# Loading the attention output matrix as two half loads, 64 rows outermost, in a two-layer hybrid kernel

## The chip, the cores and the metric

The program runs on one core of a Trainium2 chip. TensorE multiplies matrices, VectorE and ScalarE read its results out of PSUM, GpSimd (POOL) does elementwise work from SBUF, and SyncE (SP) only issues transfers; ScalarE issues transfers too, between its own instructions. Sixteen DMA engines carry all transfers. Every engine runs its instructions in their written order and waits on semaphores. The metric is the device time in microseconds. Each of the kernels is timed in several runs, and one execution is taken with the hardware profiler.

## What is computed

Two layers act on 2048 latent tokens and 256 context tokens of width 1024. Layer 0 is windowed attention with 16 heads of 64 and a SiLU gate, layer 1 a bidirectional diagonal state-space layer with a gated output. The matrix of this document, `w_out` of layer 0, is used in one line of the reference, after the attention:

```
q, k, v, z = jnp.split(h @ w_in, [...], axis=-1)
p = jax.nn.softmax(jnp.concatenate([s_win, s_ctx, s_sink], axis=-1), axis=-1)
o = (jnp.einsum('bnkgqj,bnjkd->bnqkgd', p[..., :nw], vw)
     + jnp.einsum('bnkgqc,bckd->bnqkgd', p[..., nw:nw + n_ctx], vc))
y = (o * jax.nn.silu(z)) @ w_out
```

## The kernel before

All matrix products are made of three float32r products of split operands: each tile is split into a high part, made by a copy (line 106 on ScalarE, 108 on VectorE), and a low part, the difference (line 111 on GpSimd or VectorE). A scheduler sets each engine's order of instructions when the program is built; the transfers of SyncE and ScalarE share eight completion semaphores, so a transfer also waits for an earlier one that holds its semaphore.

Phase 1 (up to about 590 us) walks over units of `w_in`: for each unit of 256 columns (keys, values, queries, gate) a raw tile `wraw` is loaded and split, and 24 products per output tile (lines 116 to 118, tile `mm`, four PSUM buffers) run over chunks of 384 tokens. ScalarE takes the gate tiles `z` out of PSUM (line 574) and stores them to `zd`. Beside the last units VectorE and ScalarE compute the tables of layer 1 (`pwe`, `pwg`, lines 240 to 380), which are stored to `tabd` with waits in between. Phase 2 is the attention: keys `kall` and `kctx`, queries `qta` and `qtb`, values `vt` and `vc` are loaded again from HBM, scores `S` (line 898) go through mask and maximum on VectorE (line 911), the exponential on ScalarE (line 912), a scaling on GpSimd (line 933), transposes on TensorE (line 947), a split (951, 952) and the product with the values (`ov`, line 967). The output product with `w_out` (line 1009) fills TensorE between these.

`w_out` is taken in eight tiles of 128 rows by 1024 columns. Rows of a tile are not adjacent in HBM: tile `kt` holds 64 rows of one head on its upper 64 partitions and 64 rows of another head, 256 rows further, on the lower 64. `wo_src` (line 491) builds this view of HBM with dimensions 2, 1, 64 and 1024: the outermost one counts the two heads. One transfer moves a whole tile, or half of its columns. The tiles are loaded at three places, always from SyncE:

- Four tiles of 512 KB into `wraw`, by `wo_early` at line 638, in two pairs between the loads of the last two units. ScalarE makes their high parts into `hhl` (three) and `adaq` (one), GpSimd the low parts.
- Two tiles of 512 KB into `wor`, also at line 638, between the loads of mask and sink and those of `qtb` and `kall`. ScalarE copies them into `wraw`.
- Two tiles as four transfers of 256 KB into `ogh` and `ogl`, at line 816, after the first gate tiles `zt` of phase 2 and ahead of `x`, `gate` and the next values. ScalarE copies them into `whi` and `wlo`, GpSimd and VectorE make the low parts.

ScalarE runs these copies in order with the reads of PSUM that TensorE waits for.

Of the kernel before, what the change touches and what calls it, by code (L numbers as in the profile page):

```python
# [16 lines left out]
D = 1024  # L17
# [68 lines left out]
class Net:  # L86
# [401 lines left out]
                self.split(hv, lv, raw[:, s].rearrange("p k (e f r) -> p f k e r", e=n, f=2)[:, f], "v", lo_eng)  # L488
        return hi, lo

    def wo_src(self, kt):
        wo = self.a["attn_w_out"][0].rearrange("(v a g d) n -> a d v g n", v=2, a=2, g=4, d=64)
        return wo[:, :, kt // 4, kt % 4]

    def phase1(self):
        nc, a = self.nc, self.a
# [3 lines left out]
        with ExitStack() as es:  # L500
# [27 lines left out]
            h = {}  # L528
# [104 lines left out]
            def wo_early(slots, raw=None):  # L633
                if raw is None:
                    raw = pb.tile([128, KT, 256], F32, name="wraw", bufs=2).rearrange("p k c -> p (k c)")
                for j, (hi, lo) in enumerate(slots):
                    c = slice(j * D, (j + 1) * D)
                    nc.sync.dma_start(raw[:, c], self.wo_src(len(self.wo)))
                    self.split(hi, lo, raw[:, c], "a", "g")
                    self.wo.append((hi, lo))  # L640

# [40 lines left out]
            for n, (half, (kind, x)) in enumerate(units):  # L682
# [25 lines left out]
                if n == 17:  # L708
                    t = pb.tile([128, 2, KT, CH], F32R, name="hhl2").rearrange("p a k c -> p (a k c)")
                    s2 = [[t[:, (j * 2 + i) * D:(j * 2 + i + 1) * D] for i in range(2)] for j in range(3)]  # L710
                    wo_early(s2[:2])
                if n == 18:
                    t = pb.tile([128, 2, 4, 256], F32R, name="adaq", bufs=1).rearrange("p a k c -> p a (k c)")
                    wo_early([s2[2], [t[:, 0], t[:, 1]]])
                    self.ada_cols(1, sm, self.ada_ps(ps2), self.g1, self.s1)
                    esm.close()
                    wts[19] = w_of(19)
                    for c in chunks:
                        if c == 5:
                            self.zlate = v_later(c, w) + z_later(c, wts[19], 3)  # L720
                        else:
                            if c == 3:
                                v_unit([c], w)
                            z_unit([c], wts[19], 3, False)
                            if c == 4:
                                v_unit([c], w)
                        if c == 3:
                            e3.close()
                            self.phase2_keys(zp)
                            pst = es.enter_context(self.pool("p1st"))  # L730
                            ts = [pb.tile([128, KT, 256], F32R, name="wraw", bufs=2).rearrange("p k c -> p (k c)") for _ in range(2)]
                            wo_early([(t[:, 0:D], t[:, D:2 * D]) for t in ts], pst.tile([128, 2 * D], F32, name="wor"))
                    break
# [54 lines left out]
    def phase2(self):  # L788
        nc, a = self.nc, self.a
        kall, pb = self.kall, self.pb  # L790
        with ExitStack() as es:
# [14 lines left out]
            def wtile(name, shape, dt, n):  # L806
                i = turn[name] = turn.get(name, -1) + 1
                return late[0].tile(shape, dt, name=f"{name}{i % n}", bufs=1)
# [3 lines left out]
            def load_wo(kt):  # L812
                for h in range(2):
                    t = wtile(("ogh", "ogl")[h], [128, 4, 128], F32R, 4).bitcast(F32).rearrange("p a b -> p (a b)")
                    wraw[kt, h] = t
                    nc.sync.dma_start(t, self.wo_src(kt)[:, :, h * 512:(h + 1) * 512])

            def split_wo(kt):
                t = pb.tile([128, KT, 256], F32R, name=("whi", "wlo")[kt - 6])
# [212 lines left out]
            def open_late():  # L1032
                while zlate:
                    fill(1)
                self.esd.close()
                late.append(es.enter_context(self.pool("p2l", 1)))
                for nm in LO.split():
                    late[0].tile([128, sizes.get(nm[:2], 512)], F32, name=nm, bufs=1)
                load_z(2, 0)
                load_z(2, 1)  # L1040
                for kt in range(6, KT):
                    load_wo(kt)
                load_x(2)
                for r in range(2):
                    gates[r] = wtile("gate", [128, D], F32, 2)
                    nc.sync.dma_start(gates[r], dap(self.modd[0], r * 3 * D + 2 * D, [[0, 128], [1, D]]))
# [975 lines left out]
```

## Time and profile before

| | us |
|---|---|
| median of three runs | 2732.37 (2731.87 to 2736.12) |
| profiled execution | 2733.07 |
| span of its instructions | 2731.3 |
| TensorE busy in the span | 2545.3 (93%) |
| VectorE, ScalarE, GpSimd busy | 1621.8, 1187.9, 938.6 |
| mean granted TensorE clock | 0.970 |

The profiled execution's own time is 1.8 us over its span. A granted clock of 1.00 is 2.4 GHz and 0.50 is 1.2 GHz. In the timeline, the idle time of an engine ahead of an instruction and what ended it stand in square brackets; an entry such as ACTq or SPq is a transfer being issued, not the transfer. A wait is put down to what came last by the profile. The row of a stretch gives its bounds and length, then the busy time (with the count of instructions) of TensorE's products, TensorE's weight loads, VectorE, ScalarE and GpSimd, the granted clock, the mean busy share of the 16 DMA engines, and GB/s.

### The profile page before, as it was taken

The page shows a single profiled execution, that of the slowest core. Times are in us where ns is not written, and L with a number is a line of the kernel's source. Part 1 is how long each engine was busy: PE and PEld are TensorE (multiplying, and loading weights), DVE is VectorE, ACT ScalarE, POOL GpSimd, SP SyncE. Part 2 cuts the span into 40 slices and gives each one's busy share as a digit, 9 for nine tenths or more (in the row PEclk, how much of TensorE's full clock was granted, in tenths as well). Part 3 has the DMA queues.
Part 4 walks back from the last instruction along what each step waited for, and adds up shares of the span by engine and source line. Part 5 has one row for each costly group of instructions (what it writes and reads, how often), then busy time and mean ns, then how long its engine had stood idle before and what let it go on. Part 6 is the DMA issues. An engine that isn't in the chain of part 4 may idle for free. (4 is left out here: it accounts for less than half of the span.)

```text
span 2731.3 us, 43882 instructions
## 1 busy us (share of the span) xinstructions
PE 2545.3 (93%) x15973; PEld 2279.4 (83%) x15973; DVE 1621.8 (59%) x3816; ACT 1187.9 (43%) x2711; POOL 938.6 (34%) x778
## 2 busy tenths in 40 slices
PE   7999999975799999999899999999679999999998
PEld 5999989875688899999799988889657778888887
DVE  4763377513798888888732168699986440001454
ACT  3201310123677777777644347734179830001221
POOL 0312332102445445455522154256255231212121
PEclk9999999988899999999999999999889999999999
DMA  8555446355454444344273100245223332223542
GB/s 281 169 170 149 151 151 179 116 149 147 106 132 108 106 101 112 85 111 101 89 191 105 63 24 24 76 135 162 80 71 96 103 84 67 80 62 99 180 146 85
DMA packets 374030, 317.22 MB, mean 116 GB/s; under 512 B 63910, under 2 KB 327094, under 8 KB 373814
## 3 DMA queue, kind: packets, MB, share of 16 engines
q1 hardware_dynamic: 264422, 235.64, 31.0%
q10 hardware_dynamic: 109392, 78.76, 9.0%
q8 instruction: 127, 2.08, 0.3%
q14 instruction: 89, 0.73, 0.1%
HBM read 225.63 MB, written 88.70 MB: 115 GB/s over the span
## 5 line engine op out<-in xcount | busy, mean ns | idle before, releaser
L116 PE MATMUL mm<-hhl,whi 128*128 128x384 f32 x848 | 288.2, 343 | 8.6 <-ACT z L574 4.1
L117 PE MATMUL mm<-hhl,whi 128*128 128x384 f32 x848 | 288.2, 340 | 0.4 <-POOL hhl L111 0.4
L933 POOL TENSOR_SCALAR P<-P,ri 128x640 f32<-128x640 f32 (+2 forms) x272 | 208.5, 780 | 230.9 <-DVE ri L931 190.0
L118 PE MATMUL mm<-hhl,wlo 128*128 128x384 f32 x848 | 286.3, 338 | 0.0
L952 DVE TENSOR_TENSOR pl<-pt,ph 128x512 fp32r<-128x512 f32 (+1 forms) x384 | 233.1, 607 | 37.8 <-ACT ph L951 34.0
L911 DVE CUSTOM_DVE_ANT_0 P<-S,mask,sink 128x640 f32<-128x640 f32 (+1 forms) x240 | 209.0, 871 | 58.1 <-PE S L902 52.4
L951 ACT ACTIVATE ph<-pt 128x512 fp32r<-128x512 f32 (+1 forms) x384 | 202.6, 528 | 75.2 <-PE pt L947 72.5
L947 PE MATMUL pt<-ident,P 128*128 128x128 f32 x1312 | 213.5, 276 | 11.9 <-POOL P L933 7.0
L912 ACT ACTIVATE P<-P,nm 128x640 f32<-128x640 f32 (+1 forms) x256 | 208.1, 813 | 22.2 <-DVE nm L911 6.6
L947 PEld LDWEIGHTS pt<-ident,P 128*128 128x128 f32 x1312 | 157.8, 141 | 30.0 <-POOL P L933 13.1
L116 PEld LDWEIGHTS mm<-hhl,whi 128*128 128x128 f32 x848 | 160.4, 190 | 19.6 <-issue 10.8
L111 POOL TENSOR_TENSOR wlo<-wraw,whi 128x512 fp32r<-128x512 f32 x60 | 86.6, 1471 | 258.9 <-DVE whi L108 252.7
L117 PEld LDWEIGHTS mm<-hhl,whi 128*128 128x128 f32 x848 | 161.2, 190 | 7.1 <-issue 6.1
L118 PEld LDWEIGHTS mm<-hhl,wlo 128*128 128x128 f32 x848 | 160.9, 190 | 0.8 <-issue 0.4
L117 PE MATMUL zps<-zh,wzh 128*128 128x256 f32 x512 | 146.0, 286 | 5.3 <-POOL zh L111 5.3
L116 PE MATMUL zps<-zh,wzh 128*128 128x256 f32 x512 | 145.8, 286 | 2.4 <-ACT wzh L106 1.1
L1851 DVE TENSOR_TENSOR gy<-gps,gs 128x512 f32<-128x512 f32 x32 | 22.1, 691 | 208.4 <-POOL gs L1849 208.4
L118 PE MATMUL zps<-zh,wzl 128*128 128x256 f32 x512 | 145.6, 285 | 0.0
L1424 DVE TENSOR_TENSOR sall<-sall 128x64 f32<-128x64 f32 x560 | 137.5, 301 | 0.1
L1848 ACT ACTIVATE gs<-gps 128x512 f32<-128x512 f32 x32 | 19.1, 596 | 259.6 <-PE gps L118 259.6
L967 PE MATMUL ov<-ph,vt 128*128 128x256 f32 x368 | 98.3, 283 | 21.9 <-DVE oT L979 21.9
L111 POOL TENSOR_TENSOR zh<-zraw,zh 128x512 fp32r<-128x512 f32 x61 | 81.9, 1350 | 101.1 <-ACT zh L106 77.8
(591 smaller groups left out, 7703.8 us busy)
## 6 DMA issues: line engine op xcount, KB each, us to landing
qta<-qd SPq DMA_DIRECT2D x144, 128.0 KB
qtb<-qd SPq DMA_DIRECT2D x144, 128.0 KB
wraw<-in_w_ada_dram SPq DMA_DIRECT2D x16, 1024.0 KB
zraw<-h1d SPq DMA_DIRECT2D x64, 256.0 KB
wraw<-in_attn_w_in_dram SPq DMA_DIRECT2D x12, 1024.0 KB
mq<-qqd SPq DMA_DIRECT2D x64, 192.0 KB
qd<-oh ACTq DMA_DIRECT2D x48, 192.0 KB
qd<-ol ACTq DMA_DIRECT2D x48, 192.0 KB
```

The source lines that it names most:

```text
L111: (nc.gpsimd if lo_eng == "g" else nc.vector).tensor_tensor(lo, src, hi.bitcast(F32), op=OP.subtract)
L116: nc.tensor.matmul(ps, whi(k), mhi(k), start=first and k == 0, stop=False)
L117: nc.tensor.matmul(ps, whi(k), mlo(k), start=False, stop=False)
L118: nc.tensor.matmul(ps, wlo(k), mhi(k), start=False, stop=last and k == nk - 1)
L911: nc.vector.tensor_tensor_reduce(o, sc, mk, -0.125, nsink[:, h:h + 1], OP.add, OP.min, nm)
L912: nc.scalar.activation(p, p, AF.Exp, bias=nm, scale=-1.0, accum_out=SM[i][:, e:e + 1])
L933: (nc.vector if e >= CTXV else nc.gpsimd).tensor_scalar(P[i][e], P[i][e], ri[:, e:e + 1], 1.0, op0=OP.mult, op1=OP.mult)
L947: ins = nc.tensor.transpose(t[:, c - c0], P[i][e][:, k * 128:(k + 1) * 128], self.ident)
L951: nc.scalar.activation(ph[:, c0:c1], t, AF.Copy)
L952: nc.vector.tensor_tensor(pl[:, c0:c1], t, ph[:, c0:c1].bitcast(F32), op=OP.subtract)
L967: self.keep("D", nc.tensor.matmul(o, v, ph[:, k * n:(k + 1) * n], start=k == 0, stop=False))
L1424: nc.vector.tensor_add(y[:, :, hs[h]], t[:, h, i], y[:, :, hs[h]])
```

## The change

Each load of a `w_out` tile is issued as two transfers, one for the upper and one for the lower 64 partitions. The view of HBM of each has 64 rows outermost. The bytes, their places in SBUF and the readers stay the same; ten transfers become twenty.

```diff
-    def wo_src(self, kt):
+    def load_wo(self, dst, kt, c):
         wo = self.a["attn_w_out"][0].rearrange("(v a g d) n -> a d v g n", v=2, a=2, g=4, d=64)
-        return wo[:, :, kt // 4, kt % 4]
+        for a in range(2):
+            self.nc.sync.dma_start(dst[a * 64:(a + 1) * 64], wo[a, :, kt // 4, kt % 4, c])
...
-                    nc.sync.dma_start(raw[:, c], self.wo_src(len(self.wo)))
+                    self.load_wo(raw[:, c], len(self.wo), slice(0, D))
...
-                    nc.sync.dma_start(t, self.wo_src(kt)[:, :, h * 512:(h + 1) * 512])
+                    self.load_wo(t, kt, slice(h * 512, (h + 1) * 512))
```

Lines after 495 stand one line later in the changed file. The scheduler orders the program anew. On SyncE, in phase 1, the two pairs of `wraw` loads stand between the loads of the value unit (`wraw_4976`) and of the last gate unit; before:

```order
L649 DMA wraw_4976<-in_attn_w_in_dram 128x8x256
L638 DMA wraw_4983<-in_attn_w_out_dram 128x1x1024 x2
L655 DMA wraw_5160<-in_attn_w_in_dram 128x8x128 x2
L638 DMA wraw_5172<-in_attn_w_out_dram 128x1x1024 x2
L655 DMA wraw_5193<-in_attn_w_in_dram 128x8x128 x2
```

and now, at the same place:

```order
L650 DMA wraw_4976<-in_attn_w_in_dram 128x8x256
L494 DMA wraw_4983<-in_attn_w_out_dram 64x1024 x4
L656 DMA wraw_5162<-in_attn_w_in_dram 128x8x128 x2
L494 DMA wraw_5174<-in_attn_w_out_dram 64x1024 x4
L656 DMA wraw_5197<-in_attn_w_in_dram 128x8x128 x2
```

Two transfers became four in each pair, and nothing else moved. On SyncE at the start of phase 2, from the mask (`z_5373`) to the keys, before:

```order
L768 DMA z_5373<-in_k_mask_dram 128x256
L772 DMA sink_5377<-in_attn_sink_dram 128x16
L638 DMA wor_5385<-in_attn_w_out_dram 128x1x1024 x2
L786 DMA qtb_5354<-qd_57 32x8x128 x8
L779 DMA kall_5351<-kd_58 32x4x384 x14
L834 DMA vt2_5552<-vd_59 128x512
L834 DMA vt3_5554<-vd_59 128x512
L834 DMA vc_5556<-vd_59 128x512
L834 DMA vc_5558<-vd_59 128x512
L779 DMA kall_5351<-kd_58 32x4x384 x2
```

and now:

```order
L769 DMA z_5377<-in_k_mask_dram 128x256
L773 DMA sink_5381<-in_attn_sink_dram 128x16
L494 DMA wor_5389<-in_attn_w_out_dram 64x1024 x4
L787 DMA qtb_5358<-qd_57 32x8x128 x8
L780 DMA kall_5355<-kd_58 32x4x384 x6
L835 DMA vt2_5558<-vd_59 128x512
L835 DMA vt3_5560<-vd_59 128x512
L835 DMA vc_5562<-vd_59 128x512
L835 DMA vc_5564<-vd_59 128x512
L780 DMA kall_5355<-kd_58 32x4x384 x10
```

The four loads of values moved ahead of eight of the loads of keys. On ScalarE, where the last four pieces of `w_out` are copied (`whi`, `wlo`) among the exponentials of the first block of phase 2, before:

```order
L106 ACTIVATE whi<-ogh_5933 128x512
L951 ACTIVATE ph<-pt 128x512
L912 ACTIVATE P,sm<-P,nm 128x512
L106 ACTIVATE whi<-ogl_5935 128x512
L106 ACTIVATE wlo<-ogh_5937 128x512
L106 ACTIVATE wlo<-ogl_5939 128x512
L951 ACTIVATE ph<-pt 128x512
L978 ACTIVATE oc<-ov 64x256
```

and now:

```order
L106 ACTIVATE whi<-ogh_5939 128x512
L952 ACTIVATE ph<-pt 128x512
L913 ACTIVATE P,sm<-P,nm 128x512
L106 ACTIVATE whi<-ogl_5942 128x512
L106 ACTIVATE wlo<-ogh_5945 128x512
L952 ACTIVATE ph<-pt 128x512
L979 ACTIVATE oc<-ov 64x256
L106 ACTIVATE wlo<-ogl_5948 128x512
```

The last copy moved behind one split and one read of the value product. TensorE's order differs in two rows of the later gate projection, GpSimd's not at all; VectorE's differs at these places and, with the same instructions, around the scan of layer 1.

## Rows read from the trace of the kernel before

**Rows 1.** Page, GB/s moved in 40 slices of the span.

```profile
GB/s 281 169 170 149 151 151 179 116 149 147 106 132 108 106 101 112 85 111 101 89 191 105 63 24 24 76 135 162 80 71 96 103 84 67 80 62 99 180 146 85
```

**Rows 2.** Stretches: busy time by engine, granted clock, DMA share, GB/s.

```profile
500.00:706.00 206.00, 139.11 (x825) 133.74 (x823) 75.77 (x225) 57.36 (x108) 35.36 (x28) 0.83 0.48 140
524.00:529.00 5.00, 3.73 (x22) 3.41 (x20) 4.93 (x27) 0.00 (x0) 0.00 (x0) 1.00 0.13 52
706.00:760.00 54.00, 53.16 (x376) 49.36 (x374) 48.12 (x129) 43.33 (x105) 27.94 (x32) 1.00 0.35 90
1955.00:1990.00 35.00, 1.01 (x8) 0.81 (x7) 35.00 (x216) 1.54 (x3) 1.40 (x2) 0.55 0.03 12
```

**Rows 3.** TensorE's waits between 500 and 706 us: total, times, longest.

```profile
PE S L898 <- DVE nm L911: 18.5, 1, 18.5
PE ov L967 <- DVE oT L979: 17.7, 2, 16.6
PE mm L116 <- ACT z L574: 16.5, 3, 9.4
PE pt L626 <- DVE pl L952: 5.2, 1, 5.2
PE pt L947 <- POOL P L933: 4.0, 2, 3.8
PE mm L116 <- DVE whi L108: 3.6, 1, 3.6
```

**Rows 4.** ScalarE's timeline, copies of `w_out`: start, duration, idle before.

```profile
530.30 1.06 ACT L106 ACTIVATE hhl<-wraw 128x1024 fp32r<-128x1024 f32 x1 [9.07 <-DMA wraw<-in_attn_w_out_dram]
...
562.74 1.06 ACT L106 ACTIVATE adaq<-wraw 128x1024 fp32r<-128x1024 f32 x1 [9.14 <-DMA wraw<-in_attn_w_out_dram]
...
623.13 1.06 ACT L106 ACTIVATE wraw<-wor 128x1024 fp32r<-128x1024 f32 x1 [10.30 <-DMA wor<-in_attn_w_out_dram]
633.74 1.06 ACT L106 ACTIVATE wraw<-wor 128x1024 fp32r<-128x1024 f32 x1 [9.55 <-DMA wor<-in_attn_w_out_dram]
...
679.74 0.63 ACT L106 ACTIVATE whi<-ogh 128x512 fp32r<-128x512 f32 x1 [4.37 <-DMA ogh<-in_attn_w_out_dram]
...
697.46 0.63 ACT L106 ACTIVATE wlo<-ogl 128x512 fp32r<-128x512 f32 x1 [5.85 <-DMA ogl<-in_attn_w_out_dram]
```

**Rows 5.** SyncE's timeline: when transfers are issued, time until the last issue.

```profile
2.63 1.03 SPq L199 DMA_DIRECT2D adaw<-in_w_ada_dram  x2
...
506.32 1.13 SPq L638 DMA_DIRECT2D wraw<-in_attn_w_out_dram  x2
...
606.26 1.56 SPq L638 DMA_DIRECT2D wor<-in_attn_w_out_dram  x2
608.51 26.45 SPq L786 DMA_DIRECT2D qtb<-qd  x8
...
670.76 0.54 SPq L816 DMA_DIRECT2D ogh<-in_attn_w_out_dram  x1
```

**Rows 6.** TensorE's timeline: first use of a load; end of a pause.

```profile
8.06 1.93 PE L166 MATMUL adap<-adaw,cs 128*32 128x256 f32 x16 [2.99 <-DMA adaw<-in_w_ada_dram]
...
638.07 0.58 PE L898 MATMUL S<-kall,qta 128*128 128x256 f32 x1 [18.45 <-DVE nm L911]
```

**Rows 7.** VectorE's timeline: splits of weights, and the mask.

```profile
529.94 2.35 DVE L111 TENSOR_TENSOR wlo<-wraw,whi 128x1024 fp32r<-128x1024 f32 x2
...
586.92 1.42 DVE L108 CAST whi<-wraw 128x512 fp32r<-128x512 f32 x4
...
611.62 0.23 DVE L769 CAST mask<-z 128x128 bf16<-128x128 f32 x1 [19.86 <-DMA z<-in_k_mask_dram]
```

**Rows 8.** Sums over half-clock stretches, three up to 583 us, four after.

```profile
sum 17.10, PE 11.53 PEld 11.53 DVE 7.56 ACT 8.84 POOL 5.31; mean PE 3.84 PEld 3.84 DVE 2.52 ACT 2.95 POOL 1.77
...
sum 54.60, PE 19.88 PEld 18.82 DVE 19.47 ACT 16.75 POOL 13.74; mean PE 4.97 PEld 4.71 DVE 4.87 ACT 4.19 POOL 3.43
```

**Rows 9.** A wait of ScalarE between 500 and 710 us.

```profile
ACT P L912 <- DMA kall<-kd: 6.0, 1, 6.0
```

## The prediction

> **What bounds the kernel now.** I read the page first, then the busy time by stretches, TensorE's waits, and the timelines of ScalarE and SyncE at the three places that load `w_out`. From 706 us on TensorE is busy 53.16 of 54 us; between 500 and 706 us it works only 139.11 of 206, at a mean granted clock of 0.83 [rows 2]. So this stretch, the seam of phases 1 and 2, loses 66.9 us to idling. Its waits name ScalarE, VectorE and GpSimd, not transfers [rows 3]; the transfers stand one step further back. ScalarE runs in order, and at each copy of a `w_out` tile it stands still until the tile has landed: 9.07 us at 530.30, 9.14 at 562.74, 10.30 and 9.55 at 623.13 and 633.74, and four waits of 3.3 to 5.9 us between 675.4 and 697.46, of which the first and last are shown [rows 4]. Behind it wait the reads of PSUM, and so TensorE.
>
> Why these loads are late: two tiles issued at 606.26 are usable at 623.13 and 633.74 [rows 4, 5], 10.6 us apart, so 512 KB moves at 49 GB/s. Between 524 and 529 us, when little but such a load moves, the DMA share is 0.13 at 52 GB/s [rows 2], and 0.13 is 2 of 16 engines. The view has outermost dimension 2. The other loads of the kernel have 32 or more rows outermost, and the first slice moves 281 GB/s [rows 1]. Transfers behind them suffer as well: the eight `qtb` loads, issued from 608.51, take 26.45 us to get out [rows 5], because part of each queues on the two busy engines and holds its semaphore.
>
> **What the change does to a load.** With 64 rows outermost on both sides I expect each half to spread over all 16 engines. Price of a 16-engine load that the trace shows: two loads of 1 MB are issued from 2.63 and the first is in use at 8.06 [rows 5, 6], so 1 MB takes at most 5.4 us from issue to use, and 1.05 MB at 281 GB/s takes 3.7. A pair of tiles is 1.05 MB. I take 5.4 for a pair on an idle queue and 3.7 behind other work; before, the first pair took 530.30 - 506.32 = 24.0. Below, a pair cannot go under the 3.7; above, the price of before stays the bound.
>
> The Trainium skill speaks on both sides here. Its page "DMA: Bandwidth & Descriptors", section "Rules for kernel authors", says that a transfer split into two partition halves gains nothing, since both halves run on the same engines; the same section says that an outermost dimension smaller than 16 confines a transfer to that many engines. The share of 0.13 agrees with the second. By the first the time would stay at 2732, which is a rival below.
>
> **The sum, place by place.** Times are positions in the trace of before.
>
> Place 1, `wraw`. The first pair now lands by about 512, so the wait of 9.07 us at 530.30 goes [rows 4]. The second pair is written over a raw tile whose last split on VectorE ends at 529.94 + 2.35 = 532.3 [rows 7]; it can be issued then, and lands at 532.3 + 5.4 = 537.7. From its last copy (562.74, [rows 4]) to the split that gives TensorE the last gate unit's weights (586.92, [rows 7]) runs a chain of table work, its stores and VectorE: 24.2 us. I let it run at the same length: 537.7 + 24.2 = 561.9 instead of 586.92, 25.0 earlier. Cross-check: TensorE's waits here are 16.5 + 3.6 = 20.1 [rows 3], and of 11.53 us of work at half clock half can come back, 5.8 [rows 8], 25.9 in all. So a pause of 1 to 2 us stays, where the table chain takes the place of the load. I take 24.
>
> Place 2, `wor`. The mask, issued just ahead, is in use at 611.62 [rows 7], so what is queued before is then through; 3.7 more for the pair gives 615.3 instead of 633.74. TensorE restarted at 638.07 after 18.45 us [rows 6], 4.3 after the last copy began; 615.3 + 4.3 is 619.6, just where it had stopped. As TensorE gains up to 3 us of clock on SyncE on the way there, I leave 2.5 of the 18.5: 16. The next wait, 5.2, stands behind ScalarE's 6.0 us at a store that needs the semaphore of a `kall` load [rows 3, 9]. The queue no longer starts 25 us late, but it still has 26 loads to move, so I leave 1.3: 3.9. Here the new order helps too: the values, needed first, stand ahead of eight key loads.
>
> Place 3, `ogh` and `ogl`. ScalarE wants the first piece at 679.74 - 4.37 = 675.37. Issued from 670.76 on, eight halves, with two gate tiles just ahead, are through by 677 to 678 instead of 697.4. The waits are 17.7 + 4.0 = 21.7 [rows 3]; I leave 3.5 (of the 17.7, one wait is 16.6; the other, 1.1, belongs to other work): 18.2.
>
> Clock. After 586 us TensorE works 19.88 us at half clock, in four stretches that follow the pauses [rows 8]; half, 9.9, can come back. The pauses that I leave may bring some of it again; I leave a third: 6.6.
>
> Added: ten more issues of about 0.5 us on SyncE (1.13 for two, 1.56 for two, [rows 5]), 5 us in all. They stand where SyncE waited up to 26 us for semaphores; I cost them at nothing, and at 5 us where that cover is gone. VectorE's new order around the scan of layer 1, where VectorE is busy 35.00 of 35 us and TensorE waits [rows 2], holds the same instructions; nothing, give or take 1.
>
> Sum: 24 + 16 + 3.9 + 18.2 + 6.6 = 68.7. From 706 us on TensorE waits for little and all loads follow its buffers, so the gain stays to the end. Against the profiled execution, 2733.1 - 68.7 = 2664.4; that execution is 0.7 over the median, so I predict **2664**.
>
> **Rivals.**
> - *Something else holds the seam back.* The loads are fast, but the transfers of phase 2's start (about 6 MB from `wor` to the last values and keys) or the table chain become the bound. For it: ScalarE's stores share semaphores with these loads [rows 9]. Against it: 206 us at 281 GB/s would carry 58 MB, and 140 GB/s, 29 MB, was asked [rows 2]. Price: place 2 and its clock are halved and place 1 loses 10: 12 + 10 lost, so 2686.
> - *The change does not do what it says.* The halves still run on few engines, and the time stays: 2732. For it, that both go through the same queue; against it, the other loads of 32 and more rows.
> - *Slower.* The halves stay slow and now hold four of eight semaphores instead of two; ScalarE's stores, which follow its reads of PSUM, then wait at each pair, as in rows 9. It decides if a half still takes about 10 us. Price: 5 us of issues and one wait of 6.0 us more: 2743.
>
> **How the numbers follow.** Forecast 0.78, own range 2652 to 2680; held back 0.18; no effect 0.02; slower 0.02. The floor is set by TensorE never idling and never at half clock between 500 and 706: 66.9 + 15.7 = 82.6, so 2650. The range 2650 to 2690 takes in the second case. A measurement of this kernel tells a change of about 0.2%, 5 us, from none: faster 0.96, within it 0.02, slower 0.02.
>
> **What would show it right or wrong.** Right: ScalarE's waits for `in_attn_w_out`, 9 to 10 us each at places 1 and 2, shrink to under 2; the `qtb` loads leave within 6 us of the first; TensorE's wait at line 898 shrinks from 18.5 to under 4 and that at line 967 from 17.7 to under 4; the half-clock stretches between 590 and 680 shrink. A pause at line 116 behind VectorE's split, at about 560, would show the table chain. Wrong: ScalarE still waits 5 us or more for a half, or TensorE waits as long behind `kall`, `vc` or a store.

## The result, and the profile after

The changed kernel takes **2674.31 us** (median of 4 runs, 2671.54 to 2675.75) against 2732.12 (4 runs, 2731.29 to 2736.12) on the same chip: a ratio of 0.9784 (95% interval 0.9769 to 0.98), 57.8 us less. Its profiled execution has a span of 2673.5 us at a mean clock of 0.979. The forecast was 2664 in a range of 2650 to 2690: the direction, the places and most of the sizes hold, 10.9 us of the 68.7 are missing.

ScalarE's copies of `w_out`, with the idle time before each in brackets (as [rows 4]):

```profile
512.51 1.06 ACT L106 ACTIVATE hhl<-wraw 128x1024 fp32r<-128x1024 f32 x1 [0.45 <-DMA wraw<-in_attn_w_out_dram]
536.81 1.06 ACT L106 ACTIVATE hhl<-wraw 128x1024 fp32r<-128x1024 f32 x1 [5.68 <-DMA wraw<-in_attn_w_out_dram]
539.05 1.06 ACT L106 ACTIVATE adaq<-wraw 128x1024 fp32r<-128x1024 f32 x1 [0.81 <-DMA wraw<-in_attn_w_out_dram]
589.14 1.06 ACT L106 ACTIVATE wraw<-wor 128x1024 fp32r<-128x1024 f32 x1 [0.95 <-DMA wor<-in_attn_w_out_dram]
591.11 1.06 ACT L106 ACTIVATE wraw<-wor 128x1024 fp32r<-128x1024 f32 x1 [0.91 <-DMA wor<-in_attn_w_out_dram]
```

The waits of 9 to 10 us are under 1. The wait of 5.68 us at 536.81 is one for the first half of a pair, which was 13.85 us before: the pair is issued only at 532.21, when its buffer is free, and ScalarE stands ready by then. For `ogh` and `ogl` no wait is left. On SyncE (as [rows 5]; start, time until the last issue):

```profile
532.21 2.39 SPq L494 DMA_DIRECT2D wraw<-in_attn_w_out_dram  x4
...
581.71 3.95 SPq L494 DMA_DIRECT2D wor<-in_attn_w_out_dram  x4
586.90 6.98 SPq L787 DMA_DIRECT2D qtb<-qd  x8
```

Four issues take 2.39 us where none waits, and the `qtb` loads leave within 7 us instead of 26.45 (6 had been said). TensorE's waits from 500 to 642 us, the stretch that was 500 to 706 (as [rows 3]: total, times, longest):

```profile
PE pt L948 <- DVE pl L953: 3.3, 1, 3.3
PE ov L968 <- DVE oT L980: 3.0, 3, 1.3
PE mm L116 <- DVE whi L108: 2.7, 1, 2.7
PE pt L627 <- DVE pl L953: 1.4, 1, 1.4
...
PE S L899 <- DVE nm L912: 1.1, 1, 1.1
```

18.5 became 1.1, 17.7 became 3.0, 16.5 for `z` is gone. To weigh the prediction's terms, the same four parts of TensorE's program stand below in each kernel (bounds and length, then busy time of TensorE's products, its weight loads, VectorE, ScalarE and GpSimd, granted clock, DMA share, GB/s): from about 501 us to the end of place 1, on to the end of the pause of place 2, the stretch of the next wait, and place 3; then all behind about 1334 us. Before:

```profile
501.32:587.45 86.13, 66.08 (x365) 63.67 (x363) 40.88 (x130) 20.65 (x26) 15.54 (x8) 0.90 0.39 120
587.45:638.05 50.60, 32.13 (x200) 31.56 (x200) 6.80 (x19) 6.36 (x12) 4.69 (x2) 0.80 0.50 147
638.05:671.87 33.82, 28.39 (x187) 27.99 (x188) 15.31 (x47) 17.13 (x41) 6.86 (x10) 0.85 0.74 193
671.87:729.40 57.53, 33.74 (x222) 30.79 (x221) 33.36 (x86) 32.16 (x77) 18.06 (x20) 0.79 0.43 119
1333.79:2722.40 1388.61, 1310.04 (x7973) 1141.60 (x7972) 722.08 (x1599) 561.13 (x1241) 461.11 (x302) 0.97 0.33 96
```

After:

```profile
500.10:563.14 63.04, 60.33 (x365) 58.54 (x363) 42.26 (x130) 21.21 (x27) 16.22 (x8) 1.00 0.60 165
563.14:595.90 32.76, 31.12 (x201) 30.55 (x201) 6.86 (x19) 6.22 (x12) 4.76 (x2) 0.95 0.82 214
595.90:627.10 31.20, 25.55 (x188) 24.76 (x189) 15.00 (x47) 17.32 (x41) 6.82 (x10) 1.00 0.89 222
627.10:665.40 38.30, 32.58 (x223) 29.48 (x222) 33.98 (x86) 32.23 (x78) 18.47 (x21) 0.96 0.68 177
1270.00:2664.66 1394.66, 1315.98 (x7974) 1146.32 (x7972) 720.71 (x1599) 562.17 (x1241) 455.96 (x302) 0.97 0.33 96
```

Length less TensorE's busy time is its idling. The four parts fell from 228.08 to 165.30 us, 62.8 less; the last part is 6.0 us longer, all of it in TensorE's busy time. Two questions are left: is it the shape of the transfer, at all three places, that gave this, and where did the missing 10.9 us go?

### The profile page after: what moved, and what is told of

It reads as the page before. It is cut to its first block, busy times and chain, and to the rows that moved or that the text cites. A ratio compares the mean times of both kernels' runs of the same rounds, so it can differ in the third digit from the quotient of the medians.

```text
span 2673.5 us, 43894 instructions
## 1 busy us (share of the span) xinstructions
PE 2540.4 (95%) x15973; PEld 2273.4 (85%) x15973; DVE 1624.3 (61%) x3816; ACT 1190.1 (45%) x2711; POOL 933.2 (35%) x778
## 5 line engine op out<-in xcount | busy, mean ns | idle before, releaser
L108 DVE CAST whi<-wraw 128x512 fp32r<-128x512 f32 (+1 forms) x80 | 53.5, 719 | 106.7 <-PE mm L117 86.7
```

The lines of the kernel that those rows point to most:

```text
L108: nc.vector.tensor_copy(hi, src)
```

## Experiments: the shape, place by place

The first four keep the changed kernel's order on every engine, and its twenty transfers, but cut a tile by columns, so that each half has the outermost dimension 2 again; in all places, or in one:

```
-        for a in range(2):
-            self.nc.sync.dma_start(dst[a * 64:(a + 1) * 64], wo[a, :, kt // 4, kt % 4, c])
+        n = (c.stop - c.start) // 2
+        for j in range(2):
+            self.nc.sync.dma_start(dst[:, j * n:(j + 1) * n], wo[:, :, kt // 4, kt % 4, c.start + j * n:c.start + (j + 1) * n])
```

> Each load of w_out is still two transfers, but cut by columns: each half has all 128 partitions and an outermost dimension of 2, as before. All engines' orders are those of the changed kernel; only the source and destination of SyncE's twenty transfers differ. Theory (the 64 rows outermost make the gain, not the two transfers): each half stays on few engines, the copies of ScalarE wait 8 to 11 us again, the seam from 500 to 706 us of before keeps its length, and the time is 2732 plus what the new order costs. From the give-back of 6.5 us seen in the trace after between 1330 and 2000 us, the theory that the new order causes it expects 2738 (2735 to 2742); the rival that the order costs nothing and the give-back comes with the earlier times expects 2732 (2730 to 2734). Rival to both (two transfers on one queue run side by side and are themselves the gain): under 2700.

Measured: 2730.16 us, ratio 0.9985 (0.9972 to 0.9998). The gain is gone, so it is the shape and not the number of transfers. The new order costs nothing either: not the 2738 of the theory that it caused the give-back.

> The changed kernel, but the four wraw loads (place 1) cut by columns, outermost dimension 2; the order of every engine is that of the changed kernel. Theory (the three places add, as the prediction's sum has them): the 24.4 us that TensorE's position showed at 587 us are lost, so 2674 + 24 = 2698 (2694 to 2702). Rival (a late place 1 is partly covered: while TensorE waits, SyncE, whose next loads wait for buffers, gets ahead at places 2 and 3, so a place alone is worth less than its row): 2685 to 2692.

> The changed kernel, but the two wor loads (place 2) cut by columns, outermost dimension 2; same order. Theory of adding places: the shift of TensorE grew from 24.4 to 45 us across place 2, so 2674 + 20.5 = 2695 (2691 to 2699). Rival (partial cover): 2680 to 2688.

> The changed kernel, but the loads into ogh and ogl (place 3) cut by columns, eight transfers with outermost dimension 2; same order. Theory of adding places: the shift grew from 45 to 64.4 us across place 3, so 2674 + 19.5 = 2694 (2690 to 2698). Rival (partial cover; place 3 had waited for a late queue and not for the loads' own slowness): 2680 to 2688.

Measured: 2696.91, 2695.55 and 2693.97 us, ratios 0.9867, 0.986 and 0.9855 (each within 0.002). TensorE's longest wait from 500 to 720 us in each, place 1, 2 and 3 (three kernels, one row each):

```profile
PE mm L116 <- ACT z L580: 16.1, 3, 7.8
```

```profile
PE S L904 <- DVE nm L917: 18.4, 1, 18.4
```

```profile
PE ov L973 <- DVE oT L985: 11.0, 3, 9.7
```

Each wait is back at its own place alone; at place 3 it is split, 11.0 us here and 6.4 behind GpSimd's scaling of `P`. By the differences of the ratios, times the 2732.12 of before, the kernels stand 22.7, 20.8 and 19.4 us over the changed one, 62.9 together, and the run with all three 54.9. A ratio is good to some 5 us to either side, so the 8 us between 62.9 and 54.9 are within the noise: the places add, and the partial cover of the rivals, by which each would be worth less alone, is not seen.

Then the shape was varied, in four kernels that give a dimension of 64, 4, 8 or 16 by taking the rows of `w_out` in another order. Their product is one with permuted rows, so they show times alone. The first issues one transfer per tile, in the order of the kernel before:

```
+        self.nc.sync.dma_start(dst, wo[:, :, kt // 4, kt % 4, c].rearrange("a d n -> d a n"))
```

> Each load of w_out is one transfer again, ten in all as in the kernel before, but its source is walked with the 64 rows outermost and the two heads inside, so that the outermost dimension is 64. The rows of a tile land interleaved (row d of the upper head on partition 2d, of the lower on 2d + 1), so the output product uses a permuted matrix. Every engine's order is that of the kernel before. Theory (the outermost dimension alone makes the gain; that there are two transfers, their ten added issues and the new order of the engines are worth nothing): 2674 (2670 to 2678). Rival (the two halves are what helps): 2732. Second rival (the ten issues or the new order cost the gain that was missed, up to 10 us): 2664 to 2668.

Measured: 2680.06 us, ratio 0.9801 (0.9785 to 0.9816), 2 us above what was expected. Nearly all of the gain is there with ten transfers. The second rival, that the added issues or the new order had cost time, falls. The kernel is if anything slower than with halves: in its profile ScalarE's wait behind `kall` is one of 6.5 us and TensorE's at line 626 one of 6.4, where the halves' order, with the values ahead of ten key loads, has two of ScalarE, 2.2 and 4.6, and two of TensorE, 1.4 and 3.3.

The other three keep two halves and give each an outermost dimension of 4, 8 and 16:

```
+        src = wo.rearrange("a (d e) v g n -> a e d v g n", e=4)
+        for a in range(2):
+            self.nc.sync.dma_start(dst[a * 64:(a + 1) * 64], src[a, :, :, kt // 4, kt % 4, c])
```

> The changed kernel with two halves per tile, but the source of each half has an outermost dimension of 4 (every fourth row, 16 of them inside), so rows are permuted within a head. The order is that of the changed kernel. Theory (the outermost dimension counts the engines of a transfer): twice the rate of before, 98 GB/s, so a pair of tiles takes 10.7 us instead of 21.4. Place 1: the second pair is issued at 532.2 and lands at 543 instead of 539, 4 us lost; place 2: 592.4 instead of 591, with a queue that starts later, 2 to 5 us; place 3: 3 to 6 us. In all 9 to 15 us over the changed kernel: 2683 to 2689. Rival (any outermost dimension over 2 does, or the size of the rows decides): 2674. Rival (a half needs 16 or more to be any faster): 2730.

> As the run with 4, but outermost dimension 8 (rows permuted within a head). Theory: 196 GB/s, 5.4 us for a pair, which is near what the changed kernel's loads take between the other traffic; 0 to 4 us over the changed kernel: 2674 to 2678. Rival (16 or more are needed): above 2685.

> As the run with 4, but outermost dimension 16 (rows permuted within a head). Theory (16 is as good as 64): 2674, within 3. Its profile is also a second look at the order and the seam of the changed kernel: if the give-back after 1280 us (13 us more of half clock than before) comes with the earlier times, it is here too; if it was an accident of one execution, the span is up to 6 us shorter.

Measured: 2698.51, 2685.3 and 2676.51 us, ratios 0.9865, 0.9814 and 0.9789. The dose counts, and 16 is as good as 64. With 4 and 8 the time missed the expectation upward, and the 2685.3 of 8 touches what the rival had expected (above 2685, if a half needed 16 to be any faster). That 8 does help shows in the second pair of place 1: from its issue to the start of ScalarE's second copy it takes 26.3 us with an outermost dimension of 2, 14.2 with 4, 11.2 with 8, 6.8 with 16, and 6.8 in the changed kernel. Rows of short stretches in which little but the second pair moves, for the outermost dimensions 2 (the first run), 4, 8 and 16 (the last two numbers are DMA share and GB/s):

```profile
541.00:546.00 5.00, 5.00 (x31) 5.00 (x30) 0.79 (x1) 0.00 (x0) 0.00 (x0) 1.00 0.13 48
```

```profile
538.00:543.00 5.00, 5.00 (x31) 5.00 (x30) 4.85 (x7) 0.00 (x0) 0.00 (x0) 1.00 0.25 82
544.00:549.00 5.00, 5.00 (x30) 5.00 (x30) 0.00 (x0) 1.44 (x2) 2.40 (x1) 1.00 0.25 95
```

```profile
538.50:542.50 4.00, 4.00 (x25) 4.00 (x24) 3.86 (x6) 0.00 (x0) 0.00 (x0) 1.00 0.50 124
```

```profile
536.00:539.50 3.50, 3.50 (x22) 3.50 (x21) 3.36 (x6) 1.44 (x2) 0.61 (x1) 1.00 0.90 198
```

The share is 2, 4, 8 and nearly 16 of 16 engines. With 4, the pair is issued from 535.13 and ScalarE's two copies begin at 544.25 and 549.31:

```profile
544.25 1.06 ACT L106 ACTIVATE hhl<-wraw 128x1024 fp32r<-128x1024 f32 x1 [11.18 <-DMA wraw<-in_attn_w_out_dram]
549.31 1.06 ACT L106 ACTIVATE adaq<-wraw 128x1024 fp32r<-128x1024 f32 x1 [3.62 <-DMA wraw<-in_attn_w_out_dram]
```

A pair takes 14.2 us from issue to use, not 10.7: that was 1.05 MB at 98 GB/s alone, without the time from the issue to the first bytes, and the rate was 82 to 95. With 8 the engines in use double but the rate rises only from 95 to 124 GB/s, so the 196 that I had scaled were not reached; why is open.

## Experiments: where the missing 10.9 us went

**The changed kernel again**, no edit.

> The changed kernel itself, unedited, profiled a second time, and timed beside the next two kernels. If the 13.6 us of half clock that the first profile has over the kernel before behind 1100 us belong to that one execution, the same stretch shows 78 to 90 us of half clock here and the seam's lead is kept to within 3 us at the end; if they belong to the kernel, they are here again, 95 us or more. The seam up to 710 us repeats within 2 us (one pause of 3.3 and one of 1.4 us at about 610). Time 2672 to 2677.

Measured: 2676.01 us, ratio 0.9783 (0.9768 to 0.9797). The same parts as above, in this execution:

```profile
500.50:567.80 67.30, 60.56 (x364) 58.55 (x363) 44.57 (x130) 21.29 (x26) 15.33 (x8) 0.98 0.56 154
567.80:601.30 33.50, 31.52 (x201) 30.93 (x201) 6.82 (x19) 6.18 (x12) 4.74 (x2) 0.93 0.83 209
601.30:634.00 32.70, 26.91 (x188) 26.11 (x189) 15.00 (x47) 17.28 (x41) 6.83 (x10) 0.95 0.87 212
634.00:672.30 38.30, 32.57 (x222) 29.50 (x222) 33.98 (x86) 32.18 (x78) 18.46 (x20) 0.96 0.68 178
1277.00:2665.55 1388.55, 1309.24 (x7973) 1141.46 (x7972) 724.14 (x1599) 561.98 (x1241) 459.58 (x302) 0.97 0.33 96
```

The give-back is not there: 1388.55, as before the change. The four parts, though, are 171.80 us and not 165.30, where 2 us of difference had been expected. Both executions end within 1 us of each other for different reasons. The sums over all half-clock stretches between 1265 and 2210 us, of before, of the changed kernel's first and of its second profile:

```profile
sum 85.20, PE 47.87 PEld 38.91 DVE 77.07 ACT 24.06 POOL 31.93; mean PE 5.98 PEld 4.86 DVE 9.63 ACT 3.01 POOL 3.99
```

```profile
sum 98.80, PE 61.73 PEld 50.66 DVE 87.31 ACT 37.93 POOL 37.37; mean PE 6.86 PEld 5.63 DVE 9.70 ACT 4.21 POOL 4.15
```

```profile
sum 85.10, PE 48.29 PEld 39.68 DVE 76.19 ACT 25.27 POOL 31.20; mean PE 6.04 PEld 4.96 DVE 9.52 ACT 3.16 POOL 3.90
```

In the first profile TensorE works 13.9 us more at half clock than before, which costs half, 6.9, where 6.0 were given back. The second profile of the same program does not have it. The length of this last part, read in all fourteen profiles of this document between the same two products of TensorE, is 1388.6 us before, 1388.9 in the run cut by columns, and 1388.2 to 1394.7 in the other twelve (mean 1391.1), of which the first profile is the longest; the run with 16 outermost, which was to tell, has 1391.0. So most of the 6.0 belongs to that execution; whether some 2 us of the gain are lost here on average is open.

What made place 1 longer by 4.3 us in the second profile stands in ScalarE's stores of tables, SyncE's two loads of gate weights, and VectorE's copies. First profile:

```profile
542.25 0.37 ACTq L136 DMA_DIRECT2D tabd<-pwg  x1
...
544.52 1.10 SPq L656 DMA_DIRECT2D wraw<-in_attn_w_in_dram  x2
...
545.62 1.08 DVE L365 COPY pwg<-pi 64x1024 f32<-64x1024 f32 x1 [3.40 <-DMA tabd<-pwg]
```

Second profile:

```profile
544.07 1.00 SPq L656 DMA_DIRECT2D wraw<-in_attn_w_in_dram  x2
...
545.02 0.37 ACTq L136 DMA_DIRECT2D tabd<-pwg  x1
...
551.77 1.07 DVE L365 COPY pwg<-pi 64x1024 f32<-64x1024 f32 x1 [6.79 <-DMA tabd<-pwg]
```

Where the store is issued ahead of the two loads, VectorE goes on 3.4 us after it; where it is issued behind them, 6.8 us. TensorE's pause at line 116 behind VectorE is 2.7 us in the one and 5.1 in the other, which has 1.6 more behind ScalarE. Five other kernels here load place 1 in halves of 16 or 64 rows outermost and have the same tables, and their profiles fall into the same two groups: with the store ahead (`wor` cut by columns, 16 outermost, GpSimd's stores) VectorE waits 3.36 to 3.44 us, with the store behind (`ogh` and `ogl` cut, SyncE's stores) 6.81 and 6.78. With whole tiles, where the store stands 2 us behind the loads, it is 5.32. So the table chain, which the prediction let run at the length of before, now bounds place 1, and in halves its length takes one of two values some 4 us apart. What decides which goes first is open.

**The wait for keys.** In the first profile ScalarE stores a tile of values between two exponentials, and waits for a `kall` load that has the store's semaphore:

```profile
601.01 0.33 ACTq L136 DMA_DIRECT2D vd<-P  x1
601.67 0.72 ACT L913 ACTIVATE P<-P,nm 128x512 f32<-128x512 f32 x1 [2.24 <-DMA kall<-kd]
...
608.71 0.33 ACTq L136 DMA_DIRECT2D vd<-P  x1
609.08 0.72 ACT L913 ACTIVATE P<-P,nm 128x512 f32<-128x512 f32 x1 [4.57 <-DMA kall<-kd]
```

By the semaphores in the trace, the store at 601.01 takes that of a `kall` load issued at 596.06, and the store at 608.71 that of one issued at 602.78; the stores that GpSimd issues in the next run take others, which SyncE and ScalarE do not use.

The next two runs move the last three of these stores to another engine's queue, and nothing else:

```
-            def v_out(i, j, p, vs):
+            def v_out(i, j, p, vs, q=nc.scalar):
...
-                self.st(self.vd[i * 3 + j], vs.bitcast(F32))
+                q.dma_start(self.vd[i * 3 + j], vs.bitcast(F32))
...
-                        v_out(i, j, st[j], stage(F32R)[:, :512].rearrange("p (a d) -> p a d", a=4))
+                        v_out(i, j, st[j], stage(F32R)[:, :512].rearrange("p (a d) -> p a d", a=4), nc.gpsimd)
```

> The changed kernel, but the last three stores of values (vd from P, in the attention's first block) are issued by GpSimd and not by ScalarE; every other instruction of ScalarE, VectorE, TensorE and SyncE keeps its place. Theory (the step of the forecast that failed: ScalarE's stores wait 2.2 and 4.6 us for the semaphore of a kall load, and TensorE for ScalarE's exponentials behind them): these waits go, the pauses of TensorE of 1.4 and 3.3 us at 604 and 611 us go to under 1 in sum, and the time falls by 3 to 5 us against the changed kernel on the same chip. Rival (the exponentials are late anyway, by VectorE's maxima or by the loads of keys): under 1.5 us. Second rival (GpSimd's issue takes its place and holds the scaling of P): 0 to 4 us slower.

> The same, but the three stores are issued by SyncE, the first two ahead of the last ten kall loads and of the last one. Theory: ScalarE is as free as with GpSimd, but now SyncE waits for the rows of P before it goes on to kall and qta; the pauses of TensorE at 604 and 611 us go, and if the later keys are not needed yet the time falls by 3 to 5 us; a wait for kall or qta behind SyncE takes the place of the pauses if they are (0 to 3 us slower than the changed kernel).

Measured: with GpSimd 2671.59 us (2667.29 to 2678.93), ratio 0.977 (0.9751 to 0.9789), 4.4 under the changed kernel on the same chip; with SyncE 2678.5, ratio 0.979 (0.9772 to 0.9807). The intervals overlap that of the changed kernel, so the times alone do not settle it; the profile does. With GpSimd ScalarE has no wait for `kall` left, and of TensorE's waits for `pl`, 3.3 and 1.4, remains:

```profile
PE pt L948 <- DVE pl L953: 0.2, 1, 0.2
```

Its third stretch, between the same two products as above, is 26.99 us long and no longer 31.20 or 32.70; 1.5 us of it are idling, not 5.7 or 5.8:

```profile
598.25:625.24 26.99, 25.53 (x188) 24.91 (x189) 15.16 (x48) 18.06 (x41) 8.73 (x13) 1.00 0.97 258
```

With SyncE the wait for the rows of `P` came before the keys and `qta`, and pauses of 2.3 and 2.0 us stayed.

**Tables with two buffers**, beside GpSimd's stores:

```
-                e, g = T("pwe", 64, 16), T("pwg", 64, 16)
+                e, g = T("pw%s" % ("e", "f")[j], 64, 16), T("pw%s" % ("g", "h")[j], 64, 16)
```

> The run with GpSimd's stores of values, and in addition the tables of layer 1 have two buffers each for pwe and pwg, so that the second pair of tables need not wait until the stores of the first have landed. The larger pool also lets the scheduler start the table work later (its loads of lambda now stand just ahead of the w_out loads, 16 places further back on SyncE). Theory (the pause that stays at place 1, 2.7 us in the first and 6.8 us in the second profile of the changed kernel, is the table chain with its waits for stores): the waits of VectorE at lines 365 and 366 and of ScalarE at line 363 for tabd go, TensorE's pause at line 116 goes to under 1 us, and the time is 2 to 5 us under the run with GpSimd's stores: 2667 to 2670. Rival (the chain is as long because it starts later, and VectorE's split of the gate weights stands behind it): the pause at line 116 is 3 us or more, 2672 to 2680.

Measured: 2665.8 us (2664.13 to 2671.33), ratio 0.9755 (0.9739 to 0.9772), the lowest of all kernels here; its interval and the changed kernel's touch only from 0.9769 to 0.9772. VectorE's copies of the second pair of tables now follow the first without a wait, and the pause at line 116 behind VectorE is shorter, but it does not vanish as expected:

```profile
546.27 1.08 DVE L365 COPY pwh<-pi 64x1024 f32<-64x1024 f32 x1
```

```profile
PE mm L116 <- DVE whi L108: 1.7, 1, 1.7
PE mm L116 <- ACT z L575: 1.6, 2, 1.0
```

The two pauses are 3.3 us together, which is what the rival had said (3 or more), but the time is not the rival's. Place 1 has 3.3 us of idling all told, where the first profile of the changed kernel had 2.7. In this execution, though, the first store stood behind the two loads (546.27 against 545.32), and the three profiles of halves with one buffer in which it stood there have 6.7 to 7.7 us of idling: against those, place 1 idles 3.4 to 4.4 us less. The profile of GpSimd's stores alone had its store ahead, and its place 1 is as short (63.3 us, 64.0 here); what it has more is in the last part, 1391.9 us against 1388.2. How much of the time is the two buffers' and how much belongs to the execution stays open.

## Why the prediction was right, and which steps were off

| term | forecast | first profile | second |
|---|---|---|---|
| place 1, waits and clock | 24 | 23.1 | 18.8 |
| place 2, the pause of 18.5 | 16 | 16.8 | 16.5 |
| the next wait, for keys | 3.9 | -0.2 | -0.4 |
| place 3 | 18.2 | 18.1 | 18.1 |
| clock behind 586 us | 6.6 | 5.0 | 3.3 |
| behind 706 us | 0 | -6.0 | 0.1 |

The last row is that of the part behind about 1334 us; the part between, from 729 us on, changes by 0.2 to 0.3 us. Each number is the difference of lengths (place 1, and the last row), of idling (the next three) or of TensorE's busy time in the three stretches behind place 1 (the clock) in the rows above. With the 1.2 and 0.8 us by which the first part starts earlier, the terms give, to 0.3 us, the 57.8 and 56.9 by which the two spans are shorter.

- **The shape.** Right. 0.13 of the DMA engines was 2 of 16; with 4 and 8 outermost the share is 0.25 and 0.50. The Trainium skill, "DMA: Bandwidth & Descriptors", section "Rules for kernel authors", says that an outermost dimension under 16 confines a transfer to at most that many engines; these shares agree. The same section of the Trainium skill says that two partition halves gain nothing over one transfer, since both use the same engines. For this change the measurement differs: halves are 57.8 us faster than whole tiles of outermost dimension 2. It agrees where the whole has 64 outermost: one such transfer gave ratio 0.9801 against 0.9784 for halves.
- **Place 1.** The mechanism is right: the table chain takes the place of the load. The second pair is issued at 532.21, as forecast (532.3), and its last copy begins 6.8 us later, not 5.4. From that copy to VectorE's split of the gate unit's weights the chain took 23.5 us in the first profile (forecast 24.2) and 27.7 in the second. That the 24 came out in the first is in part luck: it needed the shorter of the two values that the chain takes now.
- **Places 2 and 3.** Right within 1 us, and undone alone they cost 20.8 and 19.4, their clock included.
- **The next wait.** Here the forecast failed. It held that the wait of 5.2 us would shrink to 1.3 as the queue no longer starts late. The idling of this stretch did not shrink (5.4 before, 5.7 and 5.8 now): ScalarE's stores share eight semaphores with the loads of queries, keys and values, and `kall` loads issued 5 and 6 us earlier still held the two that were wanted. No row stood behind the 1.3 that the forecast left of it; it took the late start of the queue for the cause. What removes the wait is to take the stores off ScalarE.
- **Clock.** Half of 19.88 us could come back and a third was held off for the pauses left; 5.0 and 3.3 us came. By the granted clock of the rows above the rest is lost at place 2 (0.95 and 0.93) and place 3 (0.96 in both), in the second profile also in the third stretch (0.95) and at place 1 (0.98). In the first profile the third stretch kept 1.00 with 5.7 us of pauses in it, so it is not shown that its pauses bring the half clock.
- **The gain stays to the end.** It holds to within some 2 us on average, not in each execution: the half clock behind 1265 us was 98.8 us in one and 85.1 in the other. That the order moved is not the cause, since the run cut by columns has the new order and lost nothing. What makes a stretch longer in one execution stays open.
- **Ten issues at nothing.** Right: the single transfers are not faster.
- **The signs.** Most of those of being right came: TensorE's waits of 18.5 and 17.7 us are 1.1 and 3.0, and the pause behind VectorE's split that would show the table chain stands at 563 us. The `qtb` loads took 7 us and not 6. By its letter, one sign of being wrong came too, ScalarE's 5.68 us for a half; that it is not a slow load shows in the 4.6 us from the issue at 532.21 to the copy at 536.81.
- **Rivals.** That something else holds the seam back came true in part: the table chain and the semaphores, together some 5 to 10 us where I had priced them at 22.

## What to carry to other kernels

Read the outermost dimension of each transfer's source, not its size: a view that puts two heads outermost moved 49 GB/s, and the 4 MB loaded so cost 58 us because an in-order engine copied behind it. A share of DMA time that is a small whole number of sixteenths was the sign of it here (0.13, 0.25, 0.50). And when a long wait goes, look for the next releaser in the same place: here stores that share semaphores with loads, and a chain through a buffer, kept what the sum had counted as gained.

## Not expected

- Eight engines moved 124 GB/s, four 95: the rate did not follow the count.
- One transfer of a whole tile with 64 outermost moved faster than two halves, in the stretch of its second pair; the halves' stretch is the second row:

```profile
535.50:538.00 2.50, 2.50 (x16) 2.50 (x15) 2.40 (x5) 1.44 (x2) 0.43 (x1) 1.00 0.73 277
```

```profile
535.00:538.50 3.50, 3.50 (x22) 3.50 (x21) 3.36 (x6) 1.44 (x2) 0.55 (x1) 1.00 0.86 187
```

- Two executions of one program differ by 4.3 us in one place, by whether a store was issued ahead of two loads of another queue or behind them.
